# A two-block mixer and MLP on one core: the pace of a background convolution, the place of one fetch and the priority of eight loads

## The chip, the cores and the metric

One core of a Trainium2 chip runs the kernel. The metric is device microseconds of one execution. The core's engines have their own instruction queues, each in order: TensorE (PE) multiplies matrices, VectorE (DVE) and ScalarE (ACT) work on cells, GpSimd (POOL) and the sync queue (SP) issue transfers here.

## The reference

```
h = RMSNorm(x);  proj = h @ w_in -> [pool 512 | GLU 2x512 | gate_a 1024 | gate_b 1024]
A: 4 groups of 128 channels: trailing mean over 2/4/8/16 frames minus the frame,
   a linear map per group, a scale, a projection to 1024 (w_po)
B: GLU -> causal depthwise convolution of width 31 -> LayerNorm -> swish -> projection (w_co)
x = x + RMSNorm((sigmoid(gate_a) * A + sigmoid(gate_b) * B) @ w_o)
x = x + RMSNorm(relu(RMSNorm(x) @ w_up)^2 @ w_down)
```

x is 2048 x 1024, float32; there is one layer.

## The kernel before

The tokens are worked on in two blocks of 1024 (b = 0 and 1; "block one" and "block two" here). Channels lie on the partitions, and a cell is 128 partitions x 1024, two channel groups of 512 tokens. Each value is split into a high and a low part (a cast on ScalarE, L218 or L225, and a subtraction on VectorE, L121), and a product is made of three matmuls for each pair, high by high, high by low and low by high. Matrix products over 2 x 2 partitions of weights and tokens are made with seven products in place of eight (class `Octet`, indices 1 to 7); each is 24 matmuls of 128x128 by 128x512. The sums and differences of weights (`minus`, tile `ws`) and of token cells (`token_parts`, tiles `tr` and `big`) that this takes are VectorE's work.

A product's accumulator (`psum`, three of them) is read out by a `sink` (L118, `block_out`) before the same accumulator is used for the next index. In `run_octets` the first fourteen products of an input group go by `START`, pairs of octet and index; octet 0 is the pooling octet (`pool_in`) and octet 1 the first GLU octet:

```
START = ((0, 1), (0, 2), (1, 2), (1, 1), (0, 5), (0, 6), (0, 3), (0, 7))
START += ((1, 6), (0, 4), (1, 5), (1, 7), (1, 3), (1, 4))
```

Cells for a product are asked for two products ahead from the fifth product on, one before that.

After each product `bg()` advances the background lanes. A `Lane` gets `rate` credits for each product and takes a step of its generator for each whole credit; a step that yields a number of 1 or more makes the lane wait that many calls less one and drops the credit left over. The steps of `conv_steps` are one tap each (L933 for the first, L937 for the other 30), then an addition to a running sum with a store. What block one's convolution has left is done as lane 0 beside block two's input products (L1600); its normalization follows. `pooling`, called at the end of the pooling octet's index 4, the tenth product, sets that lane's rate to 2.8 and adds block two's pooling lane and a second convolution lane.

All instructions go to a scheduler, which puts them into the engines' queues by priority (the order in which they were written, less the `offset` of a `tc.high_priority`) and by its own estimate of when they can run; buffers of a pool are given out in the same order. `behind` and `mark` tie the background to the product that it was written after. The pool `tr` has nine cells, used for sums and differences, squares, gate cells and, in block two, the low parts of two pooled cells.

Block two's pooled gate is `branch_a(1, ...)`: for each output cell and token half, a product of the four pooled cells (`mixed`) with `w_po`, multiplied in place by the gate cell `sad` (L124) and stored to `mad`. `gate_of` loads the gate cells, two products ahead. The pooled cells come from `fetch_spread(mxd, 1)`, called as `early()` inside block one's `out_proj`: four loads, four casts (L1072) and four subtractions. `out_proj` makes eight products of 48 matmuls, in the order (c, t) = (0, 0), (1, 0), (2, 0), (3, 0), (0, 1), (1, 1), (2, 1), (3, 1). The norm of its token half 1 (`roots`: sums on PE at L563, a root in small steps on VectorE, a spread on PE at L653) is written among the pooled gate's first products.

Of the kernel before, what the change touches and what calls it, by code (L numbers as in the profile page):

```python
# [67 lines left out]
def block_kernel(  # L68
# [35 lines left out]
    def mk(pl, tag, dt=F32, shape=(P, TB)):  # L104
        return pl.tile(list(shape), dt, tag=tag, name=nm(tag))

    def dram(tag, shape=(P, TB), dt=F32):
        return p_dram.tile(list(shape), dt, tag=nm(tag), name=nm(tag))
# [8 lines left out]
    def add(o, a, b):  # L117
        return nc.vector.tensor_tensor(o, a, b, op=ALU.add)  # L118

    def sub(o, a, b):  # L120
        return nc.vector.tensor_tensor(o, a, b, op=ALU.subtract)  # L121

    def mul(o, a, b):
        return nc.vector.tensor_tensor(o, a, b, op=ALU.mult)  # L124

    def load(o, src):
        return nc.sync.dma_start(o, src)
# [12 lines left out]
    def mark(i):  # L140
        marks[i.ins.engine] = i.ins
        return i
# [51 lines left out]
    def clear_halos():  # L194
# [6 lines left out]
    sad, sbd, mad, x1d = (  # L201
        {(b, c, t): dram(tag) for b in range(NB) for c in range(CPS) for t in (0, 1)}
        for tag in ("sad", "sbd", "mad", "x1d")
    )
# [6 lines left out]
    def col(i):  # L211
        return cst[:, i : i + 1]


    def split(src, pl, tag):
        hi = mk(pl, tag, F32R)
        lo = mk(pl, tag, F32R)
        nc.scalar.copy(hi, src)  # L218
        sub(lo, src, f32(hi))
        return hi, lo  # L220
# [59 lines left out]
    def psum(lab):  # L280
        return ps_mm.tile([P, TB], F32, tag="mm", name=nm(lab))
# [397 lines left out]
    def inv_rms_steps(ss, inv_n, tmp, lag, got):  # L679
        st = root_pe(*ss, inv_n=inv_n)  # L680
        yield lag
        yield from spread_steps(root_dve(st), tmp, lag, got)
# [33 lines left out]
    def tr(dt=F32):  # L716
        return mk(*TR, dt)
# [234 lines left out]
    def norm_steps(b, lag):  # L952

        yield 3 if b else 1
        sh, sl = split(sums[b], *TR)
        yield 3 if b else 1
        mu = mk(p_ss, "r", F32, (P, W))[:, :TB]
        y = {}

        def prefetch(c):  # L960
            y[c] = tr()
            load(y[c], yd[b, c, 0])

        for c in range(2):
            prefetch(c)
        for t in (0, 1):
            s = slice(t * T, (t + 1) * T)
            rb = mk(ps_rb, "rb", F32, (P, T))
            nc.tensor.matmul(rb, ones, sh[:, s], start=True, stop=False)
            nc.tensor.matmul(rb, ones, sl[:, s], start=False, stop=True)  # L970
            nc.scalar.activation(mu[:, s], rb, AF.Copy, scale=1.0 / CW)
        yield 1
        ss = mk(p_ss, "sm")
        for c in range(CC):
            if c + 2 < CC:
                prefetch(c + 2)
            sub(y[c], y[c], mu)
            load(yd[b, c, 0], y[c])
            sq = ss if c == 0 else tr()
            nc.scalar.activation(sq, y[c], AF.Square)  # L980
            if c % 2:
                yield 1
            if c:
                add(ss, ss, sq)
        yield lag
        r = mk(p_ss, "r", F32, (P, W))[:, :TB]
        halves = [ss[:, t * T : (t + 1) * T] for t in (0, 1)]

        def got(t, rb):
            nc.scalar.copy(r[:, t * T : (t + 1) * T], rb)  # L990

        yield from inv_rms_steps(halves, inv_c, TR, lag, got)
        prefetch(0)
        yield 1
        sg = {}
        for c in range(CC + 1):
            if c < CC:
                if c + 1 < CC:
                    prefetch(c + 1)
                mul(y[c], y[c], r)  # L1000
                sg[c] = tr()
                nc.scalar.activation(
                    sg[c], y[c], AF.Sigmoid, scale=col(C_LG + c), bias=col(C_LB + c)
                )
                nc.scalar.activation(
                    y[c], y[c], AF.Identity, scale=col(C_LG + c), bias=col(C_LB + c)
                )
            if c:
                mul(y[c - 1], y[c - 1], sg[c - 1])
                load(zd[b, c - 1, 0], y[c - 1])  # L1010
            yield 1
# [75 lines left out]
    def half(cells, t):  # L1087
        return [tuple(p[:, t * T : (t + 1) * T] for p in hl) for hl in cells]

    def ahead_by_one(keys, fetch_one, n=1):  # L1090

        coming = []
        for i, k in enumerate(keys):
            while len(coming) <= n and i + len(coming) < len(keys):
                coming.append(fetch_one(keys[i + len(coming)]))
            yield k, coming.pop(0)

    def branch_a(b, mixed, bg):


        def gate_of(k):
            sg = tr()
            load(sg, sad[(b, *k)])
            return sg

        keys = [(c, t) for c in range(CPS) for t in (0, 1)]
        for (c, t), sg in ahead_by_one(keys, gate_of, 2):
            if t == 0:
                w = load_w(w_po[c], ("po", c))
            ps = psum("A")  # L1110
            for q in (0, 1):
                i = matmuls(ps[:, q * T : (q + 1) * T], w, CC * q, half(mixed, t))
            mark(i)
            flush()
            with tc.high_priority(offset=URGENT):
                mark(mul(sg, ps, sg))
            load(mad[b, c, t], sg)
            bg()
# [34 lines left out]
    def out_proj(b, merged, halves, bg, made, early=none):  # L1153


        o, x, rbs = {}, {}, {}
        chain = None

        def make(c, t):
            mul(two(o[c, t]), two(o[c, t]), per_token(rbs[t]))  # L1160
            add(x[c, t], x[c, t], o[c, t])
            aside(x1d[b, c, t], x[c, t])
            gained(o[c, t], x[c, t], C_MPRE, c)
            return o[c, t]

        raw = lazily(make)
        for ts in halves:
            sq = {t: Squares(TR) for t in ts}
            for c in range(CPS):
                ws = [load_w(w_o[c % 2, 2 * (c // 2) + i], ("wo", c, i)) for i in (0, 1)]  # L1170
                for t in ts:
                    ps = psum("wo")
                    for i in (0, 1):
                        for k in (0, 1):
                            i_mm = matmuls(
                                ps[:, i * T : (i + 1) * T], ws[k], 4 * i,
                                cell_rhs([merged[2 * k + j, t] for j in (0, 1)]),
                                start=k == 0, stop=k == 1,
                            )
                    mark(i_mm)  # L1180
                    flush()
                    o[c, t] = mk(*BIG)
                    sq[t].add(ps)
                    gained(o[c, t], ps, C_POST, c)
                    bg()
                    if (c, t) == (2, 1):
                        early()
                    if chain is not None:
                        with behind():
                            if next(chain, 0) == 0 and c >= 2:  # L1190
                                made(raw, 2)
            for t in ts:
                for c in range(CPS):
                    x[c, t] = mk(*BIG)
                    aside(x[c, t], xt[b, c, t])

            def roots(ts=ts, sq=sq):
                def got(k, rb):
                    rbs[ts[k]] = rb

                with tc.high_priority(offset=URGENT):
                    ss = [sq[t].total() for t in ts]
                    st = root_pe(*ss, inv_n=inv_d)
                    y = root_dve(st)
                    g = spread_steps(y, None, 1, got)
                    next(g)
                yield 1
                drain(g)

            chain = roots()  # L1210

        return chain
# [258 lines left out]
    lanes = []  # L1471

    def bg():
        with behind():
            for lane in lanes:
                lane()
# [78 lines left out]
    def then(f, o, at=4):  # L1555

        was = o.run

        def run(i, *a):
            was(i, *a)  # L1560
            if i == at:
                f()

        o.run = run
        return o
# [10 lines left out]
    pi = pool_in(0, parts)[0]  # L1576
# [8 lines left out]
    rest = tail.gens  # L1585
# [4 lines left out]
    def marked(gen, k):  # L1590
        yield from gen
        done.add(k)
# [4 lines left out]
        yield from gen  # L1597

    rest = [marked(chain_of(*rest), "conv")]
    lanes += [Lane(3.2, *rest, marked(norm_steps(0, 1), "norm"))]  # L1600

    def pooling():
        lanes[0].rate = 2.8
# [4 lines left out]
    pi = pool_in(1, parts)[0]  # L1608
    g1 = glu(1, parts), gate(1, parts, 3, sad, "ga", "lows")
    run(  # L1610
        [then(pooling, pi)],
        g1[0],
        g1[1],
        gate(1, parts, 5, sbd, "gb", "sums"),
# [402 lines left out]
```

## Time and profile before

| | us |
|---|---|
| median of 3 runs | 2190.27 |
| lowest, highest | 2186.27, 2196.49 |
| profiled execution | 2191.51 |
| its span in the profile | 2189.7 |
| PE busy in it | 2159.9 |
| VectorE busy | 1610.3 |
| ScalarE busy | 1017.6 |

The profile is of one execution. Busy time is a union over an engine's instructions; the clock that a row gives is the TensorE clock that was granted, as a share of full speed. A row of the timeline merges like instructions that follow each other. Stretches are given as start:end in us from the start of the span.

### The profile page before, as it was taken

To read this page: it belongs to the slowest core of one execution; us is meant where nothing else is said; L and a number is where in the kernel's file an instruction comes from. 1 tells how busy PE (TensorE), PEld (TensorE's weight loads), DVE (VectorE), ACT (ScalarE), POOL (GpSimd) and SP (SyncE) were. 2 spreads that over 40 slices of the span, in tenths; PEclk is the share of its full clock that TensorE was granted. 3 is DMA by queue.
4 is the path that set the end of the run, shared out by engine and by line. 5 is a ranking of instruction groups with operands and counts; after the bars stand their busy time and mean duration, and the time that the engine had idled before them with its cause. 6 is when DMAs were issued, how large, how long until landed. Compare 5 with 4: busy or idle time off the path is not lost.

```text
span 2189.7 us, 24848 instructions
## 1 busy us (share of the span) xinstructions
PE 2159.9 (99%) x9582; PEld 1783.8 (81%) x9582; DVE 1610.3 (74%) x1570; ACT 1017.6 (46%) x1060; POOL 18.2 (1%) x41
## 2 busy tenths in 40 slices
PE   9999999999999999999999999999999999999997
PEld 7888888788878878888888878888888888888886
DVE  8898788998688998987757765756644746546884
ACT  6444454334543535545635775555522423334542
POOL 1000000000000000000000000000000000000000
PEclk9999999999999999999999999999999999999998
DMA  7688897678997787435787585644877875545782
GB/s 273 239 298 316 322 345 277 228 256 295 334 371 249 254 321 267 179 144 192 278 295 271 214 284 195 225 169 161 315 283 281 309 273 183 203 156 190 273 299 71
DMA packets 153943, 552.30 MB, mean 252 GB/s; under 512 B 17216, under 2 KB 17472, under 8 KB 153792
## 3 DMA queue, kind: packets, MB, share of 16 engines
q1 hardware_dynamic: 137728, 492.94, 63.3%
q10 hardware_dynamic: 12672, 46.14, 5.4%
q0 software_dynamic: 3424, 11.63, 1.6%
q8 instruction: 75, 1.23, 0.2%
q14 instruction: 44, 0.36, 0.0%
HBM read 366.00 MB, written 185.69 MB: 252 GB/s over the span
## 4 chain that ended last, share of the span: by engine, by line
PE 91%; DVE 4%; DMA 2%; issue 1%; ACT 1%; SPq 0%; DVEq 0%; ACTq 0%
PE up L268 26%; PE down L268 22%; PE wo L268 7%; PE ga L268 7%; PE glu L268 6%; PE gb L268 6%; PE rb L268 5%; PE B L268 4%; PE A L268 4%; PE pool L268 3%; DMA wl<-kept 1%; DVE y L937 1%; PE rb L563 1%; DVE big L121 1%; DMA wr<-w_in 1%
## 5 line engine op out<-in xcount | busy, mean ns | idle before, releaser
L268 PE MATMUL up<-big,wh 128*128 128x512 f32 x1792 | 480.9, 390 | 2.4 <-DVE big L121 1.6
L268 PEld LDWEIGHTS up<-big,wh 128*128 128x128 f32 x1792 | 335.7, 188 | 74.1 <-DVE big L121 2.7
L225 ACT CAST wh<-wr 128x1024 fp32r<-128x1024 f32 x199 | 209.0, 1052 | 391.3 <-PE up L268 79.3
L937 DVE SCALAR_TENSOR_TENSOR y<-v,cst,y 128x1024 f32<-128x1024 f32 x240 | 307.6, 1282 | 2.8
L268 PE MATMUL down<-big,wh 128*128 128x512 f32 x768 | 287.4, 389 | 0.0
L268 PE MATMUL up<-big,wl 128*128 128x512 f32 x896 | 276.0, 389 | 0.0
L225 ACT CAST wh<-ws 128x1024 fp32r<-128x1024 f32 x126 | 132.4, 1052 | 264.1 <-PE up L268 67.5
L268 PE MATMUL down<-tr,wh 128*128 128x512 f32 x648 | 252.1, 389 | 0.0
L268 PE MATMUL down<-big,wl 128*128 128x512 f32 x696 | 214.3, 389 | 0.0
L121 DVE TENSOR_TENSOR tr<-tr,big 128x1024 fp32r<-128x1024 f32 x100 | 120.7, 1223 | 117.3 <-ACT big L1725 115.1
L121 DVE TENSOR_TENSOR wl<-ws,wh 128x1024 fp32r<-128x1024 f32 x118 | 144.1, 1222 | 81.1 <-ACT wh L225 80.9
L268 PEld LDWEIGHTS up<-big,wl 128*128 128x128 f32 x896 | 168.1, 188 | 34.9
L121 DVE TENSOR_TENSOR wl<-wr,wh 128x1024 fp32r<-128x1024 f32 x122 | 148.7, 1220 | 55.3 <-ACT wh L225 54.5
L1725 ACT CAST big<-tr 128x1024 fp32r<-128x1024 f32 x98 | 101.2, 1050 | 165.9 <-DMA tr<-fd 137.0
L268 PEld LDWEIGHTS down<-big,wh 128*128 128x128 f32 x768 | 144.2, 188 | 29.8
L268 PEld LDWEIGHTS down<-big,wl 128*128 128x128 f32 x696 | 130.6, 188 | 27.2
L268 PEld LDWEIGHTS down<-tr,wh 128*128 128x128 f32 x648 | 121.6, 188 | 25.2
L268 PE MATMUL wo<-big,wh 128*128 128x512 f32 x480 | 128.7, 390 | 0.0
L268 PE MATMUL glu<-big,wh 128*128 128x512 f32 x464 | 125.0, 391 | 2.0 <-ACT wh L225 1.4
L268 PE MATMUL gb<-big,wh 128*128 128x512 f32 x448 | 120.0, 390 | 0.0
L268 PE MATMUL ga<-big,wh 128*128 128x512 f32 x448 | 120.0, 390 | 0.0
L268 PEld LDWEIGHTS wo<-big,wh 128*128 128x128 f32 x480 | 89.9, 188 | 18.5
(204 smaller groups left out, 3269.1 us busy)
## 6 DMA issues: line engine op xcount, KB each, us to landing
tr<-fd SPq DMA_DIRECT2D x110, 512.0 KB, 4.8
wr<-w_down SPq DMA_DIRECT2D x90, 512.0 KB, 5.8
wl<-kept SPq DMA_DIRECT2D x85, 512.0 KB, 4.6
kept<-wl SPq DMA_DIRECT2D x72, 512.0 KB, 5.9
wr<-w_up SPq DMA_DIRECT2D x64, 512.0 KB, 4.4
wr<-w_in SPq DMA_DIRECT2D x60, 512.0 KB, 5.3
fd<-tr ACTq DMA_DIRECT2D x54, 512.0 KB, 3.4
fd<-tr SPq DMA_DIRECT2D x46, 512.0 KB, 3.0
```

The source lines that it names most:

```text
L121: return nc.vector.tensor_tensor(o, a, b, op=ALU.subtract)
L225: nc.scalar.copy(hi[:, :n], src[:, :n])
L268: i = nc.tensor.matmul(ps, w[wp][:, (at + k) * P : (at + k + 1) * P], rhs[k][xp], start=start and n == 0, stop=stop and n == len(order) - ...
L563: nc.tensor.matmul(st[:, at + g : at + g + 1], ss[:, g * P : (g + 1) * P], inv_n, start=start is None or (start and g == 0), stop=stop, sk ...
L937: nc.vector.scalar_tensor_tensor(acc, v[:, k : k + TB], wk, acc, op0=ALU.mult, op1=ALU.add)
L1725: nc.scalar.copy(hi, t)
```

## The change

Three edits. The first product to the fifth of block two's input now give lane 0 four credits each, and from the end of the pooling octet's index 5 (the fifth product) 2.2, until `pooling` sets 2.8 as before. `early()` is called after product (1, 1) of `out_proj`, one product of 48 matmuls sooner. In block two the gate cells of `branch_a` are loaded at a priority raised by 150.

```diff
@@ branch_a
         def gate_of(k):
             sg = tr()
-            load(sg, sad[(b, *k)])
+            with tc.high_priority(offset=150) if b else nullcontext():
+                load(sg, sad[(b, *k)])
             return sg
@@ out_proj
-                    if (c, t) == (2, 1):
+                    if (c, t) == (1, 1):
                         early()
@@ the main sequence
-    lanes += [Lane(3.2, *rest, marked(norm_steps(0, 1), "norm"))]
+    lanes += [Lane(4, *rest, marked(norm_steps(0, 1), "norm"))]
+
+    def parting():
+        lanes[0].rate = 2.2
...
     run(
-        [then(pooling, pi)],
+        [then(pooling, then(parting, pi, 5))],
         g1[0],
         g1[1],
         gate(1, parts, 5, sbd, "gb", "sums"),
```

`then(f, o, at)` calls `f` at the end of octet `o`'s product `at` (index 4 if none is given), after that product's `bg()`.

## The prediction

> **What bounds the kernel now.** I read the page first, then the chain that ended last, the table of stretches (one for each stage), the engines' timelines inside the two stretches that stood out, and last the page's DMA issues.
>
> ```profile
> span 2189.7 us, 24848 instructions
> PE 2159.9 (99%) x9582; PEld 1783.8 (81%) x9582; DVE 1610.3 (74%) x1570; ACT 1017.6 (46%) x1060; POOL 18.2 (1%) x41
> 92.64 5.44 PE pool L268 x24
> ...
> core 0: us, PE busy (x) PEld busy (x) DVE busy (x) ACT busy (x) POOL busy (x), PEclk, DMA share, GB/s
> 296.79:340.31 43.52, 43.52 (x193) 36.04 (x192) 39.89 (x35) 22.96 (x30) 0.00 (x0) 1.00 0.98 365
> 340.31:402.35 62.04, 57.88 (x242) 46.99 (x241) 56.05 (x49) 22.19 (x22) 0.00 (x0) 0.94 0.63 214
> 402.35:465.20 62.85, 62.85 (x278) 51.97 (x277) 58.04 (x50) 23.41 (x23) 0.00 (x0) 1.00 0.75 261
> ...
> 758.40:808.40 50.00, 47.56 (x209) 38.74 (x208) 45.78 (x51) 20.92 (x26) 4.83 (x9) 0.97 0.82 310
> ```
>
> TensorE (PE) is busy for 2159.9 of 2189.7 us: 29.8 us of idle time in all. A product of 24 matmuls, back to back, takes 5.44 us, and no edit here adds or removes a product, so the change can only move time that PE loses. The stretches show where. Block one's pooled gate (296.79 on) is eight products in 43.52 us = 8 x 5.44: nothing lost. Block two's first ten input products (340.31 to 402.35) should take 54.40 and take 62.04: **7.64 lost**, with a mean clock (the column PEclk) of 0.94. The next 62.85 us lose nothing. Block two's pooled gate (758.40 to 808.40) takes 50.00 for eight products: 6.48 over 43.52, part of it the small matmuls of a norm. The three edits touch just these two stretches, so 7.64 + 6.48 = 14.1 us is the most they could return there.
>
> The first loss, in PE's timeline and then VectorE's (DVE); a bracket is idle time before the row and what ended it:
>
> ```profile
> 389.05 0.39 PE L268 MATMUL glu<-big,wl 128*128 128x512 f32 x1
> 392.09 1.40 PE L268 MATMUL pool<-big,wh 128*128 128x512 f32 x5 [2.65 <-DVE tr L118]
> 394.99 0.80 PE L268 MATMUL pool<-big,wh 128*128 128x512 f32 x1 [1.50 <-DVE big L121]
> 395.58 1.48 PE L268 MATMUL pool<-big,wl 128*128 128x512 f32 x3
> ...
> 395.00:402.35 7.35, 7.35 (x20) 5.77 (x21) 7.35 (x7) 1.04 (x1) 0.00 (x0) 0.58 0.44 145
> ...
> 346.38 2.60 DVE L937 SCALAR_TENSOR_TENSOR y<-v,cst,y 128x1024 f32<-128x1024 f32 x2
> 351.45 1.22 DVE L118 TENSOR_TENSOR tr<-pool,tr 128x1024 f32<-128x1024 f32 x1 [2.48 <-PE pool L268]
> 352.59 7.88 DVE L937 SCALAR_TENSOR_TENSOR y<-v,cst,y 128x1024 f32<-128x1024 f32 x6
> 362.98 1.23 DVE L118 TENSOR_TENSOR ws<-wr,wr 128x1024 f32<-128x1024 f32 x1 [2.51 <-DMA wr<-w_in]
> ...
> 368.62 1.23 DVE L121 TENSOR_TENSOR ws<-ws,wr 128x1024 f32<-128x1024 f32 x1 [0.76 <-DMA wr<-w_in]
> 369.76 1.28 DVE L937 SCALAR_TENSOR_TENSOR y<-v,cst,y 128x1024 f32<-128x1024 f32 x1
> ...
> 390.73 1.22 DVE L118 TENSOR_TENSOR tr<-pool,tr 128x1024 f32<-128x1024 f32 x1
> 391.86 0.80 DVE L933 TENSOR_SCALAR y<-v,cst 128x1024 f32<-128x1024 f32 x1
> 392.58 1.22 DVE L121 TENSOR_TENSOR wl<-ws,wh 128x1024 fp32r<-128x1024 f32 x1
> 393.71 1.22 DVE L121 TENSOR_TENSOR big<-tr,big 128x1024 fp32r<-128x1024 f32 x1
> ```
>
> The tenth product (pooling octet, index 4) waits twice. At 389.44 it needs the accumulator that VectorE reads out at 390.73 (L118, done 391.95): 2.65 us. After five matmuls it needs the low half of its second cell (L121 at 393.71, done 394.93): 1.50 us. Then the clock is at 0.58 for 7.35 us: (1 - 0.58) x 7.35 = 3.1 us. Together 2.65 + 1.50 + 3.1 = 7.25 of the 7.64. Both waits are on VectorE's one queue, which has no gap from 368.62 until after the second: those rows are late because of what stands ahead of them. Yet the same queue had idled 2.48, 2.51 and 0.76 us (351.45, 362.98, 368.62) earlier in the stretch: 5.75 in all.
>
> **Edit 1: the convolution steps' pace (L1600, then `parting`).** Nothing is added but order. Ten products at 3.2 were 32 credits; five at 4 and five at 2.2 are 31. A step that starts a channel group (a load, no arithmetic) spends what credit is left. Counting from the lane's start, steps traced by the end of products 3, 4, 5, 6, 7 were 9, 12, 16, 19, 21 (the sum is step 20, the load step 21), and become 12, 16, 20, 21, 23. In the before-trace the taps bear this out: one at 344.05, two at 346.38, six at 352.59 are steps 1 to 9.
>
> Three extra steps thus become available by the third product and four by the fourth. A tap in a row takes 7.88 / 6 = 1.31 us. One extra lands in the 2.48 gap (1.3 us), two in the 2.51 gap (filled), the fourth covers the 0.76: 1.3 + 2.5 + 0.76 = 4.6 us of idle used. Against that, the tenth product's cells are asked for at the eighth product, when 23 steps are traced and not 21: less the load, 22 vector operations and not 20, of which 21 in fact stood ahead of the row at 393.71. So one or two steps more, 1.2 us each among other work (368.62 to 369.76 is 1.14, a tap 1.2), 1.2 to 2.4 us. Net: the two late rows come 2.2 to 3.4 us earlier; I take 2.8. Then the accumulator is read by 389.2, before PE asks at 389.44: that wait is gone. The low half is there at 392.1, and PE wants it at 389.44 + 1.1 = 390.6: 1.5 us stay.
>
> Does 1.5 us of idle still cost clock? The rows below answer with a wait of 1.54 us: 0.54 of the clock for 3.70 us, 1.7 us of time. That is the nearest row, so I charge it. Edit 1: 7.64 - 1.5 - 1.7 = **4.4 us gained**, between 0 (the scheduler puts all four early steps ahead of the late rows without using the gaps) and 7.64. Below zero is not excluded: two more steps and no gap used is 2.4 us lost.
>
> [...]
>
> After the tenth product what is late next is the split of the next weights on VectorE, which has 58.04 us of work in the 62.85 of the stretch from 402.35. If PE comes 4.4 earlier those 4.8 of slack just cover it. Further on the convolution stands one step later (1.2 us) in a lane that nobody waits for until the normalization.
>
> **Edits 2 and 3: the pooled cells and the gate loads.** The same for block two's pooled gate:
>
> ```profile
> 669.67 54.40 PE wo L268 x240
> ...
> 747.71 0.32 SPq L127 DMA_DIRECT2D wl<-kept  x1
> 748.08 1.00 SPq L127 DMA_DIRECT2D tr<-mxd  x2
> 749.18 0.63 SPq L127 DMA_DIRECT2D wr<-w_up  x1
> ...
> 761.48 2.09 SPq L127 DMA_DIRECT2D tr<-sad  x4
> ...
> 760.47 1.22 DVE L121 TENSOR_TENSOR tr<-tr,big 128x1024 fp32r<-128x1024 f32 x1
> ...
> 767.01 1.23 DVE L124 TENSOR_TENSOR tr<-A,tr 128x1024 f32<-128x1024 f32 x1 [1.85 <-DMA tr<-sad]
> 768.15 1.22 DVE L118 TENSOR_TENSOR tr<-tr,tr 128x1024 f32<-128x1024 f32 x1
> ...
> 770.48 0.69 DVE L118 TENSOR_TENSOR tr<-tr 128x512 f32<-128x512 f32 x1
> ...
> 761.75 0.50 PE L268 MATMUL A<-tr,wh 128*128 128x512 f32 x1 [0.90 <-DVE tr L121]
> 771.31 1.02 PE L563 MATMUL rb<-inv_d,tr 128*128 128x1 f32 x8 [1.54 <-DVE tr L118]
> ...
> 773.20:776.90 3.70, 3.70 (x11) 2.86 (x10) 3.48 (x5) 1.03 (x1) 0.00 (x0) 0.54 0.66 211
> ```
>
> Edit 2 moves one call past product (2, 1): four loads, four casts on ScalarE, four subtractions on VectorE. Two of the loads (into `tr`) are issued by the sync queue (SP) at 748.08. Asked one output product earlier (48 matmuls; 240 take 54.40 in the first row, so 10.9 us), they can leave earlier by anything from 0 (their `tr` buffers not free) to 10.9. The last subtraction (760.47) ends at 761.69 and PE waits 0.90 us for it; 3 us earlier is enough, so 0.90 goes. What the four subtractions (4.9 us) push back on VectorE is the convolution and the scaling of the MLP's first cells, first used after this stretch's eight products: more than 40 us of cover. On SP the two loads pass the w_up load at 749.18 and little else.
>
> Edit 3: the first gate loads are issued at 761.48, and the first product, done at about 764.7 (758.40 + 5.44 + 0.90), is multiplied by them only at 767.01, after 1.85 us of waiting on VectorE. Behind that sit the two additions (768.15, 770.48), done at 771.17, for which PE waits 1.54 us at its sums, after which it loses (1 - 0.54) x 3.70 = 1.7 us to the clock. With the gate cells landed before 764.7 the additions end at 769.3; PE reaches that place at 769.77 (771.31 - 1.54), or 768.9 once edit 2's 0.90 is out, and VectorE is freer by the subtractions that went ahead. So 0.90 + 1.54 + 1.7 = 4.1 us can go. What is late next is the spread of that norm, some 15 us on, at the end of a chain of small steps on VectorE that would have to come just as much earlier; I keep 0.6 for it: **3.5 us gained**, between -2 and 4.8 (6.48 less some 1.7 of the norm's own small matmuls).
>
> **Sum.** 4.4 + 3.5 = 7.9. From the profiled execution's 2191.51 that is 2183.6; it stands 1.24 above the median 2190.27, from which it would be 2182.4. I say **2183.0**. The runs before spread from 2186.27 to 2196.49, so about 0.5% (11 us) is what can be told from no change; 7.9 us is 0.36%.
>
> **Rivals.**
> (a) The clock does not fall for the short wait that remains: 4.4 becomes 6.1, time 2181.3. For it is a wait elsewhere, with the clock of its stretch at 1.00:
>
> ```profile
> 604.65 0.95 PE L268 MATMUL gb<-big,wl 128*128 128x512 f32 x3 [0.69 <-DMA wl<-kept]
> 545.10:626.00 80.90, 79.65 (x358) 65.26 (x357) 54.24 (x60) 45.35 (x46) 0.00 (x0) 1.00 0.95 348
> ```
>
> Against: 0.69 us is half of what stays here, and 1.54 is all of it. [...]
>
> (b) Edit 1 does not do what it says: the scheduler orders by its own clock, the 2.51 gap was closed by a weight's landing that it believed earlier, and the extra steps fall behind it, right among the late rows. Then only 3.5 goes: 2191.51 - 3.5 = 2188.0. For it: before 393.71 taps and other rows alternate one for one, whatever the credit.
> (c) Both losses go whole: 7.64 + 4.8 = 12.4, time 2179.1 from the profiled run, 2177.9 from the median. For it: each wait missing takes its clock loss along. It needs the low half 4.3 us earlier, by more than I find.
> (d) Slower: raised by 150, all eight gate loads take `tr` buffers as they come free, and SP, in order, sits at one whose buffer is still held while the next pooled weight's low half is behind it.
>
> ```profile
> 781.73 5.76 SPq L127 DMA_DIRECT2D mad<-tr  x2
> ...
> tr<-sad SPq DMA_DIRECT2D x8, 512.0 KB, 6.8
> wl<-kept SPq DMA_DIRECT2D x12, 512.0 KB, 4.6
> ```
>
> SP did sit so for 5.76 us at a store in this stretch. With 4.6 us to land behind that, a weight wanted every 10.9 us has almost no slack: 5.8 us of PE waiting and 1.7 of clock, 7.5 each. With the two last of the four weights late it is 2191.5 - 4.4 + 15 = 2202.1, from which point on it is slower by over 0.5%; with three 2209.6. Against: the loads already run two products ahead and SP bears it; the nine `tr` buffers hold two pooled cells, so up to five gate cells leave two.
>
> **How the numbers follow.** Forecast 0.28 (2183); (a) 0.17; (b) 0.21; (c) 0.20; (d) 0.14. The range leaves out (d) and the tail below (c): 2176 (2177.9 less scatter) to 2197 (2188.0 or no gain at all, 2190.3, with the scatter up to the highest run before, 2196.49). Faster by over 0.5% is below 2179.3: (c) and a little of (a), 0.24. Slower is above 2201.2: (d), 0.14. The rest, 0.62, within.
>
> **What would show it.** Right: seven to nine taps in a row before the row that was at 362.98 and less idle ahead of it; the ten products in 57 to 58 us, one wait of about 1.5 us left in the tenth; the two pooled loads before 745, the gate loads before 757, the wait of 1.54 gone and PEclk 1.00 over the pooled gate, which takes about 46.5 us. Wrong: the ten products still at 62; PE waiting for `wl<-kept` in the pooled gate; a new wait in the products after 402 or in the first MLP products; PE losing time outside these stretches.

## The result, and the profile after

The changed kernel takes 2183.07 us (median of 20 runs, 2177.95 to 2187.70), the kernel before 2189.48 over as many runs: ratio 0.9972, 95% interval 0.9965 to 0.9978. That is 6.4 us faster, within 0.5%. Its profiled execution, at 2187.70, was the slowest of the twenty, so a second one of the same program is read beside it (the run `e8_changed_again`; at 2180.86 it was in turn the fastest of that run's eight).

Of the first profile, the page's head, the stretches that answer to those of before, PE's rows with a wait, and the loads on the sync queue with the multiplication that waits for them:

```profile
span 2185.9 us, 24843 instructions
PE 2158.2 (99%) x9582; PEld 1783.0 (82%) x9582; DVE 1610.6 (74%) x1570; ACT 1017.9 (47%) x1060; POOL 18.2 (1%) x41
...
340.36:400.57 60.21, 56.72 (x241) 45.81 (x241) 55.77 (x49) 22.43 (x23) 0.00 (x0) 0.97 0.64 218
755.73:805.42 49.69, 47.67 (x210) 38.97 (x210) 44.68 (x51) 18.91 (x25) 4.85 (x9) 0.97 0.87 324
767.02:770.50 3.48, 3.48 (x9) 2.75 (x10) 2.63 (x5) 0.00 (x0) 0.48 (x1) 0.56 0.39 159
...
350.65 1.65 PE L268 MATMUL pool<-big,wl 128*128 128x512 f32 x3 [3.16 <-DMA wl<-kept]
394.83 1.64 PE L268 MATMUL pool<-big,wh 128*128 128x512 f32 x6 [0.29 <-DVE tr L118]
765.90 1.11 PE L563 MATMUL rb<-inv_d,tr 128*128 128x1 f32 x8 [2.02 <-DVE tr L118]
...
734.17 1.53 SPq L127 DMA_DIRECT2D tr<-mxd  x2
755.98 0.32 SPq L127 DMA_DIRECT2D wl<-kept  x1
756.36 5.52 SPq L127 DMA_DIRECT2D tr<-sad  x6
...
763.94 1.23 DVE L124 TENSOR_TENSOR tr<-A,tr 128x1024 f32<-128x1024 f32 x1 [1.21 <-DMA tr<-sad]
```

The tenth product waits 0.29 us in place of 2.65 and 1.50, and the clock stays whole there (1.00 from 353.69 to 766.69). The ten products still take 60.21 us, because the second of them waited 3.16 us for a weight that landed late, with the clock at 0.50 from 350.27 to 353.68 (a mean of 0.97 over the ten). The pooled gate of block two has hardly changed: 49.69 us in place of 50.00, a wait of 2.02 us before its sums in place of 0.90 and 1.54, and the clock at 0.56 for 3.48 us. The two pooled loads leave at 734.17, 21.6 us ahead of the gate's start in place of 10.3, but the gate loads only right behind a weight load at 755.98, when the first product has already begun.

The second profile of the same kernel; first its stretches (the ten products, the pooled gate, and the time behind the sums), then PE's two rows with a wait, then VectorE's queue in the ten products:

```profile
339.94:394.98 55.04, 54.78 (x242) 44.99 (x241) 52.55 (x45) 21.35 (x22) 0.00 (x0) 1.00 0.64 217
749.94:797.64 47.70, 45.80 (x210) 37.55 (x209) 44.40 (x50) 19.14 (x24) 4.89 (x10) 1.00 0.88 333
761.00:766.00 5.00, 5.00 (x23) 4.12 (x24) 4.50 (x9) 1.96 (x3) 0.53 (x1) 1.00 0.49 154
...
389.44 1.63 PE L268 MATMUL pool<-big,wh 128*128 128x512 f32 x6 [0.26 <-DVE tr L118]
760.09 1.02 PE L563 MATMUL rb<-inv_d,tr 128*128 128x1 f32 x8 [1.90 <-DVE tr L118]
...
345.15 3.92 DVE L937 SCALAR_TENSOR_TENSOR y<-v,cst,y 128x1024 f32<-128x1024 f32 x3
351.19 1.22 DVE L118 TENSOR_TENSOR tr<-pool,tr 128x1024 f32<-128x1024 f32 x1 [2.12 <-PE pool L268]
352.33 10.52 DVE L937 SCALAR_TENSOR_TENSOR y<-v,cst,y 128x1024 f32<-128x1024 f32 x8
362.77 1.22 DVE L118 TENSOR_TENSOR ws<-wr,wr 128x1024 f32<-128x1024 f32 x1
...
388.07 1.22 DVE L118 TENSOR_TENSOR tr<-pool,tr 128x1024 f32<-128x1024 f32 x1
389.27 1.23 DVE L121 TENSOR_TENSOR big<-tr,big 128x1024 fp32r<-128x1024 f32 x1
390.41 1.28 DVE L937 SCALAR_TENSOR_TENSOR y<-v,cst,y 128x1024 f32<-128x1024 f32 x1
391.61 1.22 DVE L121 TENSOR_TENSOR wl<-ws,wh 128x1024 fp32r<-128x1024 f32 x1
```

Here the ten products take 55.04 us, where ten times 5.44 is 54.40, and the wait of 3.16 us is absent: it belongs to that execution, not to the change. VectorE shows edit 1 as it was meant: three taps in a row where two stood, eight where six stood, and no idle time before the row at 362.77 (2.51 us before). The last four rows are the readout of the accumulator, the low half, a tap and a weight's low half. In the kernel before, a tap and a weight's low half stood between the first two.

### The profile page after: what moved, and what is told of

Same layout as the page of the kernel before. It is cut to its first block, busy times and chain, and to the rows that moved or that the text cites. A ratio compares the mean times of both kernels' runs of the same rounds, so it can differ in the third digit from the quotient of the medians.

```text
span 2185.9 us, 24843 instructions
## 1 busy us (share of the span) xinstructions
PE 2158.2 (99%) x9582; PEld 1783.0 (82%) x9582; DVE 1610.6 (74%) x1570; ACT 1017.9 (47%) x1060; POOL 18.2 (1%) x41
## 4 chain that ended last, share of the span: by engine, by line
PE 89%; DVE 5%; DMA 3%; ACT 1%; issue 1%; SPq 0%; DVEq 0%
PE up L268 26%; PE down L268 22%; PE wo L268 7%; PE ga L268 7%; PE gb L268 7%; PE rb L268 5%; PE glu L268 5%; PE B L268 4%; PE pool L268 2%; PE A L268 2%; DVE y L937 1%; DMA big<-xt 1%; DVE big L121 1%; DMA wl<-kept 1%; PE rb L563 1%
## 5 line engine op out<-in xcount | busy, mean ns | idle before, releaser
L268 PE MATMUL up<-big,wh 128*128 128x512 f32 x1792 | 481.0, 390 | 2.3 <-DVE big L121 1.6
L268 PEld LDWEIGHTS up<-big,wh 128*128 128x128 f32 x1792 | 335.7, 188 | 74.1 <-DVE big L121 2.7
L268 PE MATMUL down<-big,wh 128*128 128x512 f32 x768 | 287.4, 389 | 0.0
L268 PE MATMUL up<-big,wl 128*128 128x512 f32 x896 | 276.1, 389 | 0.0
L268 PE MATMUL down<-tr,wh 128*128 128x512 f32 x648 | 252.1, 389 | 0.0
L268 PE MATMUL down<-big,wl 128*128 128x512 f32 x696 | 214.2, 389 | 0.0
L268 PEld LDWEIGHTS up<-big,wl 128*128 128x128 f32 x896 | 168.1, 188 | 34.8
L268 PEld LDWEIGHTS down<-big,wh 128*128 128x128 f32 x768 | 144.2, 188 | 29.9
L268 PEld LDWEIGHTS down<-big,wl 128*128 128x128 f32 x696 | 130.6, 188 | 27.2
L268 PEld LDWEIGHTS down<-tr,wh 128*128 128x128 f32 x648 | 121.7, 188 | 25.2
L268 PE MATMUL wo<-big,wh 128*128 128x512 f32 x480 | 128.7, 390 | 0.0
L268 PE MATMUL glu<-big,wh 128*128 128x512 f32 x464 | 125.4, 391 | 1.2 <-ACT wh L225 0.7
L268 PE MATMUL gb<-big,wh 128*128 128x512 f32 x448 | 120.0, 390 | 0.0
L268 PE MATMUL ga<-big,wh 128*128 128x512 f32 x448 | 120.0, 390 | 0.0
L268 PEld LDWEIGHTS wo<-big,wh 128*128 128x128 f32 x480 | 89.9, 188 | 18.5
```

Of the source, the lines that this page charges most:

```text
L268: i = nc.tensor.matmul(ps, w[wp][:, (at + k) * P : (at + k + 1) * P], rhs[k][xp], start=start and n == 0, stop=stop and n == len(order) - ...
```

## The experiments

Two theories went into the first three runs. P: the pace of edit 1 carries the whole change, and edits 2 and 3 give almost nothing. S: the split of the prediction, 4.4 and 3.5 us. The first run names a third, N, that the gain comes from the pooled gate. Gains in us below are worked out from the ratio, not from the two medians.

**Edit 1 alone**

```diff
-    lanes += [Lane(3.2, *rest, ...)]
+    lanes += [Lane(4, *rest, ...)]
+    def parting():
+        lanes[0].rate = 2.2
-        [then(pooling, pi)],
+        [then(pooling, then(parting, pi, 5))],
```

> Edit 1 alone. Theory P (the pace carries the change): ten products in 54.5 to 56.5 us, no half clock in the tenth, the pooled gate of block two as before at 50.0 us; 6 us under the kernel before, ratio 0.997. Theory S (the split of the prediction: 4.4 from the pace, 3.5 from the other two): 4.4 us under it, ratio 0.998. Theory N (the gain comes from the pooled gate): under 1 us, ratio 1.000.

Measured: ratio 0.9971 (0.9961 to 0.9981), 6.4 us. The stretches of the ten products and behind the sums, and PE's waits:

```profile
340.02:396.44 56.42, 55.30 (x241) 44.65 (x240) 54.94 (x47) 21.71 (x22) 0.00 (x0) 1.00 0.66 229
766.90:773.00 6.10, 6.10 (x23) 4.90 (x23) 5.21 (x9) 1.05 (x1) 0.00 (x0) 0.72 0.63 188
...
390.89 1.62 PE L268 MATMUL pool<-big,wh 128*128 128x512 f32 x6 [0.57 <-DVE tr L118]
766.26 1.02 PE L563 MATMUL rb<-inv_d,tr 128*128 128x1 f32 x8 [1.82 <-DVE tr L118]
```

The ten products take 56.42 us at a clock of 1.00; the pooled gate keeps its wait (1.82) and its slow clock (0.72 over 6.10 us). P holds: the one edit gives what all three give. N falls; S, with 0.998, stands at the edge of the interval.

**Edit 2 alone**

```diff
-                    if (c, t) == (2, 1):
+                    if (c, t) == (1, 1):
                         early()
```

> Edit 2 alone. Theory P: the wait of 0.90 us goes, but the scheduler sets the sums of the norm nine matmuls (2.0 us) sooner on PE, so their wait grows from 1.5 to some 2.5 us and the clock still halves: within 1 us of the kernel before, ratio 1.000. Theory S: 1 to 2 us under it, ratio 0.9993.

Measured: ratio 0.9994 (0.9983 to 1.0005), not told apart from none, nor P from S. PE's wait at the sums and the stretch behind it:

```profile
767.75 1.02 PE L563 MATMUL rb<-inv_d,tr 128*128 128x1 f32 x8 [1.73 <-DVE tr L118]
768.00:773.00 5.00, 5.00 (x26) 4.25 (x27) 4.53 (x7) 1.32 (x2) 0.53 (x1) 1.00 0.70 228
```

The 0.90 us wait is gone, but the scheduler set the sums earlier. In the queue order on PE they stand after 35 of the stretch's matmuls with edit 2 and after 44 without it, and they wait 1.73 us in place of 1.54, less than the 2.5 of theory P. The clock did not fall this time (1.00 over 5.00 us).

**Edit 3 alone**

```diff
-            load(sg, sad[(b, *k)])
+            with tc.high_priority(offset=150) if b else nullcontext():
+                load(sg, sad[(b, *k)])
```

> Edit 3 alone. Theory P: the first four gate loads keep their place behind the same weight load on the sync queue, and only the fifth and sixth move, ahead of a store: no change, ratio 1.000. Theory S: the wait of 1.54 us and the half clock go, 3.2 us under the kernel before, ratio 0.9985.

Measured: ratio 1.0001 (0.9990 to 1.0012). The sync queue and PE's wait:

```profile
762.17 0.38 SPq L127 DMA_DIRECT2D wl<-kept  x1
762.61 8.26 SPq L127 DMA_DIRECT2D tr<-sad  x6
...
772.43 1.02 PE L563 MATMUL rb<-inv_d,tr 128*128 128x1 f32 x8 [1.41 <-DVE tr L118]
```

Six gate loads leave together where four did, still directly behind the same weight load (762.17). The priority moved the fifth and the sixth; the four that count did not go sooner, and the wait stays, 1.41 us, this time with the clock whole (1.00 from 772.90 to 778.00). What held the four no run isolates. Theory S, which had 0.9985, falls with this run.

**Half of edit 1, twice**

```diff
-    lanes += [Lane(3.2, *rest, ...)]
+    lanes += [Lane(4, *rest, ...)]
```

> Only the first half of edit 1: four credits for each of the ten products, no 2.2. Theory G (the gain needs both halves: early steps that fill VectorE's idle time, and then fewer steps ahead of the late rows): 24 steps stand ahead of the accumulator's readout in place of 22, so it comes about 3.6 us later than with edit 1, PE waits about 4 us in the tenth product and the clock halves: within 1.5 us of the kernel before, ratio 0.9995 to 1.001. Rival E (filling the early idle time is what pays): as edit 1, ratio 0.997.

```diff
+    def parting():
+        lanes[0].rate = 2.2
-        [then(pooling, pi)],
+        [then(pooling, then(parting, pi, 5))],
```

> Only the second half of edit 1: 3.2 credits as before, 2.2 from the fifth product's end. Theory G: 20 steps ahead of the readout as in the kernel before, the early idle time of about 5 us unused; only one short step leaves the place between the readout and the cell's low half: the waits of 2.65 and 1.50 us become about 2.65 and 0.7, under 1.5 us gained, ratio 0.9993 to 1.000. Rival L (fewer steps late is what pays): as edit 1, ratio 0.997.

Measured: four throughout 0.9999 (0.9985 to 1.0012); the late slack alone 1.0058 (1.0045 to 1.0070), 13 us slower. First the former's ten products and its wait in the tenth, then the latter's, with the two largest waits further on and the clock behind each:

```profile
339.20:399.20 60.00, 56.28 (x241) 46.13 (x241) 57.86 (x50) 22.26 (x23) 0.00 (x0) 0.97 0.61 208
392.10 1.77 PE L268 MATMUL pool<-big,wh 128*128 128x512 f32 x6 [3.72 <-DVE tr L118]
```

```profile
339.83:397.79 57.96, 55.24 (x241) 44.81 (x240) 53.00 (x46) 22.24 (x22) 0.00 (x0) 1.00 0.64 224
391.17 1.38 PE L268 MATMUL pool<-big,wh 128*128 128x512 f32 x5 [1.78 <-DVE tr L118]
393.35 0.50 PE L268 MATMUL pool<-big,wh 128*128 128x512 f32 x1 [0.79 <-DVE big L121]
...
769.96 1.82 PE L563 MATMUL rb<-inv_d,tr 128*128 128x1 f32 x8 [2.85 <-DVE tr L118]
770.00:776.00 6.00, 6.00 (x18) 5.09 (x19) 3.64 (x6) 0.00 (x0) 0.00 (x0) 0.50 0.74 262
...
1014.90 1.06 ACT L980 ACTIVATE tr<-tr 128x1024 f32<-128x1024 f32 x1 [1.86 <-DVE tr L121]
1017.17 1.06 ACT L980 ACTIVATE tr<-tr 128x1024 f32<-128x1024 f32 x1 [0.28 <-DVE tr L121]
1018.14 0.99 ACT L439 COPY tr<-up 128x1024 f32<-128x1024 f32 x1
1019.19 2.93 PE L268 MATMUL up<-big,wh 128*128 128x512 f32 x6 [4.53 <-ACT tr L439]
1019.19:1022.60 3.41, 3.41 (x8) 2.73 (x9) 3.41 (x4) 0.88 (x1) 0.00 (x0) 0.50 0.97 395
```

Neither half does it: both are needed, as theory G has it. With four throughout, 24 steps stand ahead of the readout and it makes PE wait 3.72 us. Its profiled execution, at 2182.59, was the fastest of twelve with a median of 2187.99, so this profile shows the wait but not where the median's other time goes. With the slack alone the waits are 1.78 and 0.79, and the run loses what neither theory had: five convolution steps are missing by the tenth product (25 in place of 30, by the lane's rule), and the loss comes later, in waits of 2.85 us before the sums and 4.53 us in the first block's MLP, each with the clock at 0.50 behind it. At the second, squares of a convolution's normalization (L980) stand on ScalarE right ahead of the readout (L439) that PE waits for, the later of them after idle time of its own. The sums, too, stand earlier on PE in this run, after 34 of the gate's matmuls in place of 44. That the missing steps did both is how I read it; no run isolates it. If it is so, the 4 does a second thing: it pays in advance for the 2.2.

**The first gate cell with the pooled cells.** In the changed kernel:

```diff
+    FIRST, first = ((0, 0),), {}
...
         def gate_of(k):
+            if b and k in first:
+                return first[k]
...
+    def both_fetched():
+        fetched.extend(fetch_spread(mxd, 1))
+        for k in FIRST:
+            first[k] = tr()
+            load(first[k], sad[(1, *k)])
```

`out_proj` gets `both_fetched` as its `early`.

> The changed kernel, and the first gate cell of block two's pooled gate is loaded with the pooled cells, right behind them. Theory P: the first multiplication no longer waits 1.2 us for its load, the sums wait under 1 us in place of 2.0, the clock stays whole: pooled gate in 46 to 47 us in place of 49.5, 3 us under the changed kernel (ratio to the kernel before 0.9955). Rival: the sums then wait for VectorE's own queue just as long, or the clock halves for any wait there: within 1 us of the changed kernel, 0.997.

Measured: ratio 0.9960 (0.9945 to 0.9975). Since that overlaps the changed kernel's, both were run again side by side.

> The changed kernel as it is, beside the next one on the same chip: ratio to the kernel before 0.9965 to 0.9978, as measured. In its profile the sums of block two's pooled gate wait 1.7 to 2.1 us; whether the clock halves there may differ from the first profile, as it did between the runs so far.

> The changed kernel with the first gate cell loaded along with the pooled cells, once more. If the load of that cell is what the sums wait for: a wait of 0.6 us, no half clock, 1.4 us under the changed kernel where its clock stays whole and up to 3.1 where it halves: ratio to the kernel before 0.9955 to 0.9965. Rival: the first measurement was scatter, ratio 0.997 like the changed kernel.

Measured: the changed kernel 0.9976 (0.9965 to 0.9986), with the first cell 0.9960 (0.9946 to 0.9973), medians 2184.15 and 2180.52. Twice the same 0.9960, 1.2 thousandths below the changed kernel's first figure and 1.6 below its second; the intervals still touch, so it is likely, not certain, that this version beats both. Side by side, five of its six times lie below seven of the changed kernel's eight. The load, the multiplication, the sums and the pooled gate of its second profile:

```profile
732.56 0.72 SPq L127 DMA_DIRECT2D tr<-sad  x1
759.29 1.21 DVE L124 TENSOR_TENSOR tr<-A,tr 128x1024 f32<-128x1024 f32 x1
761.25 1.02 PE L563 MATMUL rb<-inv_d,tr 128*128 128x1 f32 x8 [0.64 <-DVE tr L118]
752.51:799.00 46.49, 45.85 (x210) 37.60 (x209) 44.31 (x50) 18.63 (x25) 4.84 (x9) 1.00 0.90 333
```

The cell is asked for at 732.56, its multiplication waits for no load, and the sums wait 0.64 us. The pooled gate takes 46.49 us at a clock of 1.00.

**The sums later.** In the changed kernel, the chain of the norm starts one pooled product later:

```diff
-        if n[0] <= 3:
+        if n[0] == 1:
+            return
+        if n[0] <= 4:
             with behind():
                 next(chain, None)
```

> The changed kernel, and the norm's sums, root and spread are asked for one product later in the pooled gate (the sums stand 26 matmuls later on PE, 5.9 us; the spread three to seven). If the place of the sums alone makes the wait of 2 us and the half clock, 2 to 3.7 us under the changed kernel (ratio to the kernel before 0.9955 to 0.996). Rival: between sums and spread 36 matmuls (8.2 us) are left for a chain of small steps that took 15 us on VectorE, so the wait moves to the spread: 0 to 4 us over the changed kernel, ratio 0.997 to 0.999.

Measured: ratio 0.9967 (0.9956 to 0.9979), the changed kernel's own within the interval. The gain did not come; the rival's time nearly fits, but not its reason, since PE has no wait of 0.25 us or more in this pooled gate but the one at the sums. VectorE, PE and the stretch behind the sums:

```profile
765.91 1.22 DVE L124 TENSOR_TENSOR tr<-A,tr 128x1024 f32<-128x1024 f32 x1
767.04 0.68 DVE L118 TENSOR_TENSOR tr<-tr 128x512 f32<-128x512 f32 x1
...
767.87 1.50 PE L563 MATMUL rb<-inv_d,tr 128*128 128x1 f32 x8 [1.69 <-DVE tr L118]
768.00:776.00 8.00, 8.00 (x26) 6.57 (x27) 5.25 (x9) 0.00 (x0) 0.00 (x0) 0.57 0.80 274
```

The last addition moved along: it now stands behind the second gate multiplication (765.91), and PE waits 1.69 us for it all the same. In this run, then, setting the sums later does not remove the wait: the addition went back with them, behind a later multiplication in VectorE's queue.

## Why the prediction was right, and where it was not

The time (2183.0 forecast, 2183.07 measured) and the largest term's mechanism held; the split between the terms did not, and two errors cancelled.

- **Edit 1: 4.4 forecast, 6.4 measured.** The term that was mis-sized is what stays of the wait. In both kernels VectorE waits for PE ahead of the row at 351.45 (351.19 in the second profile), so the rows are counted from there. The readout comes 36.88 us behind that row in place of 39.28, 2.4 us earlier, and the low half 38.08 in place of 42.26, 4.2 earlier, where I had 2.8 for both. Idle time filled behind that row is 2.51 + 0.76 = 3.3 us, not 4.6, since the gap ahead of it is a wait for PE and shrank by 0.36 only. From the start 22 steps stand ahead of the low half in place of 21, one more, as forecast, and 22 ahead of the readout in place of 20; behind that row it is one more for the readout, a channel group's first, 0.72 us from its start to the next row's. That makes about 2.5 for the readout, and 1.8 more for the low half, because the tap and the weight's row that stood between the two fell behind both. I had assumed that order kept. So no 1.5 us wait remained, and no 1.7 us of clock to charge for it (the ten products' clock is 1.00 in the second profile). Rivals (a) and (c) described this product better than the forecast did; (b), that the extra steps would fall among the late rows, is refuted by the eight taps in a row.
- **Edits 2 and 3: 3.5 forecast, 1.3 and -0.2 measured, neither told apart from zero.** The step that failed is "with the gate cells landed before 764.7", which is by the end of the first product, 6.3 us behind the gate's start. They did not: in the first profile the multiplication starts 8.2 us behind the gate's start (763.94 and 755.73), after 1.21 us of waiting for its load, where it was 8.6. The priority did not move the first four loads. And the 0.90 us wait went, but the sums, set nine matmuls (2.0 us) sooner, still waited 1.73 us where I had them wait no more. I had treated PE's order as fixed while the work beside it moved.
- **What is late next** was sought in the right places but was not there: the weights behind the tenth product did not stop PE in the second profile, and PE did not wait there for the norm's spread in any run.
- **Rival (d)** did not come: the gate loads issue back to back, in 5.5 us for six, and no pooled weight made PE wait.

The 2183.0 was thus partly luck: one term too small by 2.0, the other too large by some 2.4. The gain was 6.4 us and not 7.9, and the median of the kernel before, over twenty runs, is 0.8 below that of the three that the forecast started from.

## What to carry to other kernels

When VectorE's one queue makes PE wait at a point, count the background steps ahead of that point and the idle time before it. Moving steps into that idle time paid here with 22 steps ahead of the readout in place of 20, and no longer with 24; with the total cut by five the kernel was slower. A raised priority did nothing for the four loads behind the weight load; writing the first of them down earlier did, so look at what stands in front of a transfer on its queue. After any edit to a scheduled kernel compare the queue orders themselves, because the scheduler may spend the time that you freed.

## What the runs showed of the hardware

A short wait cost clock in one execution and none in the next. In the changed kernel the sums waited 2.02 us in the first profile, and the clock behind them was 0.56 over 3.48 us; in the second they waited 1.90 us, and it was 1.00 over 5.00 us. Among the other profiles, waits at the sums of 1.54 us (the kernel before), 1.82 (`e1_pace`) and 1.69 (`e7_sums_later`) were followed by a clock of 0.54 over 3.70 us, 0.72 over 6.10 and 0.57 over 8.00; waits of 1.73 (`e2_fetch`) and 1.41 (`e3_gate`) by 1.00 over 5.00 and 5.10 us.

Between 301 and 2140 us the clock is at 0.50 in two stretches of the kernel before (394.37:401.20 and 773.25:776.66) and in two of the changed kernel's first profile (350.27:353.68 and 766.70:770.11), and at 1.00 in all the rest. PE's big matmuls (L268) alone, in that last stretch and in the 3.41 us ahead of it (the columns behind the length: PE, its weight loads, PEclk, DMA share, GB/s):

```profile
763.29:766.70 3.41, 0.59 (x3) 0.17 (x1) 1.00 1.03 419
766.70:770.11 3.41, 3.23 (x8) 2.62 (x9) 0.50 0.50 202
```

The wait and most of the sums' small matmuls fall into the first, in which the big matmuls are busy for 0.59 us of 3.41; the second is at half clock, a loss of 1.7 us. The length of the wait does not decide it alone: 1.90 us went without a loss and 1.54 with one. What does, these runs do not show.

For estimates, four of the seven waits of 1.41 to 2.02 us above were followed by a slow clock, so such a wait here should carry a chance of the clock's loss (1.7 us in the first profile, (1 - 0.57) x 8.00 = 3.4 in `e7_sums_later`), not the whole of it. This is one part of the difference between two executions of one program: the first profile's ten products and pooled gate (60.21 and 49.69 us) hold a stretch at 0.50 each, 3.4 us of loss together, and the second's (55.04 and 47.70) are at 1.00.
